# A hybrid SSD and delta-rule layer: the substitution of the 32-blocks and the decay differences on GpSimd instead of VectorE

## The chip, the cores and the metric

One core of one Trainium2 chip runs the whole kernel. The metric is the device time of one execution in microseconds (us); the time before is the median of three executions. All rows below are from one profiled execution. Engine names are those of the profile: PE is TensorE, DVE is VectorE, ACT is ScalarE, POOL is GpSimd, SP is SyncE, whose queue (SPq) issues nearly all DMAs.

## The reference, cut to what matters

The layer projects 1024 latent and 256 context tokens (2048 wide) by `w_in`, runs a depthwise convolution, and feeds half of the width to an SSD scan and half to a gated delta rule with 8 heads of 128, in both directions. The result is normalised and multiplied by `w_out`. The change touches the delta rule alone. In chunks of 128 tokens, for each head and direction:

```python
gcum = jnp.cumsum(g, axis=-1)
decay = jnp.exp(jnp.where(incl, gcum[..., :, None] - gcum[..., None, :], -jnp.inf))
a_strict = jnp.where(strict, jnp.einsum('bhcik,bhcjk->bhcij', k_beta, k) * decay, 0.0)
sol = lax.linalg.triangular_solve(a_strict, rhs, left_side=True, lower=True, unit_diagonal=True)
attn = jnp.einsum('bhcik,bhcjk->bhcij', q, k) * decay
def step(S, inp):
    qd, ke, ui, wi, ai, dec = inp
    v_new = ui - jnp.einsum('bhqk,bhkv->bhqv', wi, S)
    o = jnp.einsum('bhqk,bhkv->bhqv', qd, S) + jnp.einsum('bhqs,bhsv->bhqv', ai, v_new)
    S = S * dec[..., None, None] + jnp.einsum('bhsk,bhsv->bhkv', ke, v_new)
```

There are 10 chunks (8 latent, 2 context), so 20 triangular 128x128 matrices for each head.

## The kernel before, in words

`Layer.build` (L1201) writes the work as a list of steps and issues them in that order. `gdn_block` steps ("g") are convolution blocks: 48 matmuls for each 512 tokens (`group`, L440, L437) into a PSUM bank of the tags d (two) or e (one), then an evacuation by ACT (L490) and four DVE taps (L498), a Tanh (L502) and a DVE product (L503). The weights of a block are split into two float16 halves (L408 to L413), one block ahead. POOL scales the taps (L483).

Head h of the delta rule goes through five steps. "V" (`gdn_post`, L626) normalises. "P" (`gdn_prep`, L679) goes over the 10 chunks: a load `gb<-gr` (L686) brings the cumulated gates of both directions, broadcast over the partitions, into one of four buffers gb; `decay` (L673) subtracts the column's own gate and takes the minimum with the mask `mneg` (0 or -1e30), one DVE instruction for each direction (L676); ACT takes the exponential (L690); PE forms k·k and q·k (L693, L695) in a PSUM bank of the tag m (two); DVE makes A (L697, twice) and the attention block (L700), which is stored from gb (L701), and then gb is free for the next load. After the last chunk `invert_blocks` (L705) sends the 80 diagonal blocks of 32x32 through DRAM so that each lies on one partition (L716, L717, L721), inverts them by substitution, 30 pairs of DVE instructions (L726 a product into tp, L728 a sum into X) each of which needs the one before, writes ones on the diagonal (L729, POOL) and sends them back through DRAM (L730, L732). "I" (`invert`, L735) transposes them (L741, DVE) and builds the 128x128 inverses from them with small matmuls (L764 to L794). "C" (`gdn_chain`, L798) walks the two chains of 10 steps: S·k (L850), r (L856, DVE), the inverse times r (L866), xw (L871, DVE) and r (L873, ACT), the update of S (L876 on PE, L881 on DVE), and the output (L888 on PE, L889 on DVE); vq loads (L811, L813) feed it, and POOL scales finished pairs of outputs (L831 to L835). "E" (`gdn_end`, L895) transposes the output (L96) and stores it.

The order of steps for head h in the loop is P(h+1), C(h), the blocks of head h+2 with E(h) between them, V(h+2), z blocks, I(h+1). Within that, the framework's scheduler merges the steps: each engine's instructions stand in one fixed order, chosen when the program is built from modelled times, and at run time each engine takes them in that order and waits on semaphores. In the trace PE alternates between chain matmuls and matmuls of a convolution block, and DVE between the substitution and the chain.

Of the kernel before, what the change touches and what calls it, by code (L numbers as in the profile page):

```python
# [12 lines left out]
ALU = mybir.AluOpType  # L13

P = 128
# [18 lines left out]
NEG = -1.0e30  # L34
# [10 lines left out]
class Layer:  # L45
# [627 lines left out]
    def decay(self, e, d, h, c):  # L673

        nc = self.nc
        nc.vector.scalar_tensor_tensor(out=e, in0=e, scalar=self.G[:, 32 + d * 8 + h, c:c + 1],  # L676
                                       in1=self.mneg[:, d], op0=ALU.subtract, op1=ALU.min)

    def gdn_prep(self, h, D):  # L679
        nc, sp = self.nc, self.gp  # L680
# [24 lines left out]
    def invert_blocks(self, A):  # L705

        nc, sp = self.nc, self.gp
        t_ = lambda shape, name, **kw: sp.tile(shape, F32, tag=name, name=name, **kw)
        Q = 2 * NCH
        ft = t_([P, NCH, 32], "ft")  # L710
        d1 = self.dram.tile([Q, 4, 32, 32], F32, tag="d1", name="d1", bufs=2)
        d2 = self.dram.tile([Q, 4, 32, 32], F32, tag="d2", name="d2", bufs=2)
        for b in range(4):
            s = slice(32 * b, 32 * b + 32)
            nc.vector.transpose(out=ft[s], in_=A[s, 0, :, s])
            nc.sync.dma_start(out=d1[NCH:, b].rearrange("q j i -> j q i"), in_=A[s, 1, :, s])  # L716
        nc.sync.dma_start(out=d1[0:NCH].rearrange("q b j i -> (b j) q i"), in_=ft)  # L717

        X = t_([P, NCH * P], "X")[0:4 * Q, 0:1024].rearrange("p (a b) -> p a b", b=32)
        tp = t_([4 * Q, 256], "tp")  # L720
        nc.sync.dma_start(out=X, in_=d1.rearrange("q b j i -> (q b) j i"))  # L721
        for k in range(1, 31):
            m = 31 - k
            t = tp[:, 0:m * k].rearrange("p (a b) -> p a b", b=k)
            sh = [4 * Q, m, k]
            nc.vector.tensor_tensor(out=t, in0=X[:, k + 1:, k:k + 1].to_broadcast(sh),  # L726
                                    in1=X[:, k:k + 1, 0:k].to_broadcast(sh), op=ALU.mult)
            nc.vector.tensor_tensor(out=X[:, k + 1:, 0:k], in0=X[:, k + 1:, 0:k], in1=t, op=ALU.add)  # L728
        nc.gpsimd.memset(X.rearrange("p a b -> p (a b)")[:, ::33], 1.0)  # L729
        nc.sync.dma_start(out=d2.rearrange("q b j i -> (q b) j i"), in_=X)  # L730
        xc = t_([P, Q, 32], "xc")
        nc.sync.dma_start(out=xc, in_=d2.rearrange("q b j i -> (b j) q i"))  # L732
        return xc
# [586 lines left out]
```

## Time and profile before

| what | value |
|---|---|
| median of three executions | 2357.67 us (2355.03 to 2359.08) |
| the profiled execution's own time | 2351.73 us |
| span of the profile | 2350.0 us, mean granted TensorE clock 0.978 |
| busy PE / DVE / ACT / POOL | 92% / 60% / 42% / 11% of the span |
| the delta rule's stage (380 to 1480 us) | PE busy 1016.1 of 1100 us, DVE 775.0, ACT 441.7, POOL 160.9 |

A row of a timeline gives the start and the duration in us, engine, line, operation, output<-input, and in brackets the idle time of the engine just before and what ended it. A row of waits says who waited for whom, the us in total, how often, and the longest. A row of a group gives the count, the busy time, the mean ns of one, and the idle time before with its releasers. A row of a stretch gives its bounds and length, then the busy us (and instructions) of PE, PEld (weight loads), DVE, ACT and POOL, then the granted TensorE clock (PEclk, 1.00 is 2.4 GHz, 0.50 is 1.2 GHz), the DMA share and GB/s.

### The profile page before, as it was taken

Reading aid. Unit: us, or ns where it says so; the run is one execution under the profiler, and the core shown is the slowest. Engines: PE = TensorE matmul, PEld = TensorE weight load, DVE = VectorE, ACT = ScalarE, POOL = GpSimd, SP = SyncE. Lnnn points to the kernel's source line nnn. Section 1 sums busy time; section 2 is a strip of 40 time slices with the busy share of each in tenths; the row PEclk is TensorE's granted clock in tenths of the full one; section 3 lists DMA queues with packets and bytes.
Section 4 is the critical chain, followed back from the end, with each engine's and each line's share of the span. In section 5 each row is a group of like instructions: output and inputs, shape, how many; then the busy total and the mean of one; then the engine's idle time right before and its main releaser. Section 6 shows DMA issues by size and latency. Waiting matters only on the chain. (4 is left out here: it accounts for less than half of the span.)

```text
span 2350.0 us, 41855 instructions
## 1 busy us (share of the span) xinstructions
PE 2162.5 (92%) x16070; PEld 1379.2 (59%) x16070; DVE 1399.5 (60%) x3499; ACT 998.5 (42%) x2493; POOL 268.7 (11%) x514
## 2 busy tenths in 40 slices
PE   4989999889999898998989999999999999899998
PEld 4334644456665655556555566555555555788887
DVE  5335543869694856858568486566767773511214
ACT  6026422344444352433524444465667584423320
POOL 1000001012111020111201110130303130000000
PEclk9999999999999999999999999999999999999999
DMA  9952347454444344343443444333465355212117
GB/s 323 348 164 55 80 145 217 117 131 106 134 115 120 101 126 116 88 133 93 121 119 85 127 123 115 99 90 108 111 183 149 98 164 195 68 37 73 55 37 269
DMA packets 397236, 301.71 MB, mean 128 GB/s; under 512 B 61339, under 2 KB 358684, under 8 KB 395628
## 3 DMA queue, kind: packets, MB, share of 16 engines
q1 hardware_dynamic: 386668, 293.80, 43.7%
q10 hardware_dynamic: 10368, 5.24, 0.8%
q8 instruction: 126, 2.06, 0.4%
q14 instruction: 74, 0.61, 0.1%
HBM read 241.41 MB, written 57.57 MB: 127 GB/s over the span
## 5 line engine op out<-in xcount | busy, mean ns | idle before, releaser
L437 PE MATMUL ps_d<-u,w 128*128 128x512 f16 (+1 forms) x4560 | 969.6, 357 | 8.3 <-DVE cv L498 4.6
L437 PEld LDWEIGHTS <-w 128*128 128x128 f16 x6048 | 595.3, 100 | 494.3 <-issue 36.4
L1138 PEld LDWEIGHTS <-u 128*128 128x128 f16 x3072 | 298.7, 98 | 50.9 <-DMA u<-in_w_out_dram 13.2
L437 PE MATMUL ps_e<-u,w 128*128 128x512 f16 (+1 forms) x1296 | 314.5, 376 | 0.0
L498 DVE SCALAR_TENSOR_TENSOR cv<-ps_d,taps,cv 128x496 f32<-128x496 f32 (+3 forms) x300 | 194.8, 650 | 80.0 <-ACT cv L492 38.6
L413 DVE SCALAR_TENSOR_TENSOR w<-w,scl 128x512 f16<-128x512 f32 (+1 forms) x204 | 149.9, 777 | 50.8 <-ACT w L411 50.3
L408 ACT ACTIVATE w<-w 128x1024 f16<-128x1024 f32 (+1 forms) x102 | 106.5, 1044 | 167.7 <-DMA w<-in_w_in_dram 101.5
L1138 PE MATMUL ps_d<-wx,u 128*128 128x256 f16 x1536 | 170.2, 273 | 4.6 <-DMA u<-in_w_out_dram 4.6
L1138 PE MATMUL ps_d<-w,u 128*128 128x256 f16 x1296 | 144.8, 273 | 5.7 <-DMA u<-in_w_out_dram 3.8
L1168 DVE SCALAR_TENSOR_TENSOR raw<-ps_d,inv,gp 128x256 f32<-128x256 f32 x59 | 28.4, 483 | 193.2 <-ACT jko L1166 193.2
L411 ACT ACTIVATE w<-w,scl 128x1024 f16<-128x1024 f32 (+1 forms) x102 | 112.3, 1133 | 36.2 <-DVE scl L145 16.5
L1166 ACT ACTIVATE jko<-ps_d,inv 128x256 f32<-128x256 f32 x59 | 27.8, 471 | 182.4 <-PE ps_d L1138 177.4
L989 ACT ACTIVATE E<-E,G 128x128 f32<-128x128 f32 x256 | 80.9, 388 | 35.1 <-DMA E<-gr 29.6
L690 ACT ACTIVATE gb<-gb 128x256 f32<-128x256 f32 x80 | 32.2, 413 | 147.0 <-DVE gb L676 144.0
L502 ACT ACTIVATE t<-cv 128x512 f32<-128x512 f32 (+1 forms) x98 | 55.7, 570 | 90.0 <-DVE cv L498 75.4
L676 DVE SCALAR_TENSOR_TENSOR gb<-gb,G,mneg 128x128 f32<-128x128 f32 x160 | 50.8, 345 | 69.2 <-DMA gb<-gr 67.9
L873 ACT ACTIVATE r<-ps_c,nb 128x128 f32<-128x128 f32 x128 | 45.7, 364 | 107.0 <-DVE xw L871 97.2
L876 PE MATMUL ps_c<-xw,vq 128*128 128x128 f32 x288 | 61.8, 304 | 30.8 <-DVE xw L871 14.2
L726 DVE TENSOR_TENSOR tp<-X 80x30 f32<-80x30 f32 (+14 forms) x240 | 77.6, 323 | 13.9 <-DMA X<-d 13.2
L876 PEld LDWEIGHTS ps_c<-xw,vq 128*128 128x128 f32 x288 | 47.4, 196 | 58.9 <-ACT r L873 33.7
L503 DVE SCALAR_TENSOR_TENSOR cv<-t,cv 128x512 f32<-128x512 f32 (+1 forms) x98 | 60.5, 618 | 31.7 <-ACT t L502 31.3
L728 DVE TENSOR_TENSOR X<-X,tp 80x30 f32<-80x30 f32 (+14 forms) x240 | 78.4, 327 | 0.6
(329 smaller groups left out, 3250.4 us busy)
## 6 DMA issues: line engine op xcount, KB each, us to landing
w<-in_w_in_dram SPq DMA_DIRECT2D x102, 512.0 KB
x<-in_w_ada_dram SPq DMA_DIRECT2D x48, 1024.0 KB
vq<-vq SPq DMA_DIRECT2D x128, 256.0 KB
E<-gr SPq DMA_DIRECT2D x64, 256.0 KB
u<-in_w_out_dram SPq DMA_DIRECT2D x24, 512.0 KB
gb<-gr SPq DMA_DIRECT2D x80, 128.0 KB
x<-in_x_dram SPq DMA_DIRECT2D x8, 1024.0 KB
vq<-gb SPq DMA_DIRECT2D x64, 128.0 KB
```

What stands on the lines that cost most here:

```text
L408: nc.scalar.activation(out=w16[h][:, 0], in_=w[h], func=AF.Square, accum_out=ssq[:, h:h + 1])
L411: nc.scalar.activation(out=w16[h][:, 0], in_=w[h], func=AF.Copy, scale=t)
L413: nc.vector.scalar_tensor_tensor(out=w16[h][:, 1, s], in0=w[h][:, s], scalar=t, in1=w16[h][:, 0, s], op0=ALU.mult, op1=ALU.subtract)
L437: self.nc.tensor.matmul(out=ps, lhsT=w16[k // KH][:, a, k % KH], rhs=self.u16[b][k][:, lo:lo + n], start=(k == 0 and i == 0), stop=(k == K ...
L498: nc.vector.scalar_tensor_tensor(out=o3[:, :, lo_o:hi_o], in0=p3[:, :, lo_o + s:hi_o + s], scalar=taps[tap], in1=o3[:, :, lo_o:hi_o], op0= ...
L502: nc.scalar.activation(out=t[:, 0:n], in_=o, func=AF.Tanh)
L503: nc.vector.scalar_tensor_tensor(out=o, in0=t[:, 0:n], scalar=1.0, in1=o, op0=ALU.add, op1=ALU.mult)
L726: nc.vector.tensor_tensor(out=t, in0=X[:, k + 1:, k:k + 1].to_broadcast(sh), in1=X[:, k:k + 1, 0:k].to_broadcast(sh), op=ALU.mult)
L728: nc.vector.tensor_tensor(out=X[:, k + 1:, 0:k], in0=X[:, k + 1:, 0:k], in1=t, op=ALU.add)
L876: nc.tensor.matmul(out=pS, lhsT=vq[:, 1], rhs=xw, start=True, stop=True)
L989: nc.scalar.activation(out=E[:, d, r], in_=E[:, d, r], func=AF.Identity, bias=self.G[:, j, c:c + 1])
L1138: self.nc.tensor.matmul(out=ps, lhsT=self.y16(k, p, s), rhs=w16[k // 4][:, q, k % 4], start=(i == 0 and j == 0), stop=(i == KB - 1 and j = ...
```

## The change

`decay` becomes two POOL instructions, a subtraction with a minimum against 0 and an `affine_select` that writes -1e30 beyond the diagonal; and the 60 instructions of each head's substitution are issued on POOL. Nothing else is edited; the DMAs around them stay on SP.

```diff
     def decay(self, e, d, h, c):
         nc = self.nc
-        nc.vector.scalar_tensor_tensor(out=e, in0=e, scalar=self.G[:, 32 + d * 8 + h, c:c + 1],
-                                       in1=self.mneg[:, d], op0=ALU.subtract, op1=ALU.min)
+        nc.gpsimd.tensor_scalar(out=e, in0=e, scalar1=self.G[:, 32 + d * 8 + h, c:c + 1], scalar2=0.0,
+                                op0=ALU.subtract, op1=ALU.min)
+        s = 1 - 2 * d
+        nc.gpsimd.affine_select(out=e, in_=e, compare_op=ALU.is_ge, fill=NEG, base=0, pattern=[[s, P]], channel_multiplier=-s)
...
-            nc.vector.tensor_tensor(out=t, in0=X[:, k + 1:, k:k + 1].to_broadcast(sh),
+            nc.gpsimd.tensor_tensor(out=t, in0=X[:, k + 1:, k:k + 1].to_broadcast(sh),
                                     in1=X[:, k:k + 1, 0:k].to_broadcast(sh), op=ALU.mult)
-            nc.vector.tensor_tensor(out=X[:, k + 1:, 0:k], in0=X[:, k + 1:, 0:k], in1=t, op=ALU.add)
+            nc.gpsimd.tensor_tensor(out=X[:, k + 1:, 0:k], in0=X[:, k + 1:, 0:k], in1=t, op=ALU.add)
```

## Rows read from the trace of the kernel before

**Rows 1.** The page, part 1: busy time, share and instructions of each engine.
```profile
PE 2162.5 (92%) x16070; PEld 1379.2 (59%) x16070; DVE 1399.5 (60%) x3499; ACT 998.5 (42%) x2493; POOL 268.7 (11%) x514
```

**Rows 2.** Busy time by stretch, around the prep and the substitution of one head.
```profile
750.00:790.00 40.00, 31.78 (x197) 22.54 (x195) 27.38 (x83) 8.57 (x21) 0.00 (x0) 0.96 0.50 127
790.00:830.00 40.00, 38.84 (x238) 26.85 (x239) 36.78 (x129) 14.25 (x40) 10.19 (x24) 0.96 0.27 77
```

**Rows 3.** Waits of PE in the delta rule's stage, 380 to 1480 us.
```profile
PE ps_c L888 <- DVE S L881: 14.4, 7, 3.3
PE ps_c L876 <- DVE xw L871: 14.2, 5, 3.2
PE ps_c L876 <- ACT r L873: 13.4, 8, 3.0
PE ps_c L876 <- DMA vq<-gb: 3.0, 1, 3.0
```

**Rows 4.** Groups of DVE instructions that the change moves.
```profile
L728 DVE TENSOR_TENSOR X<-X,tp 80x30 f32<-80x30 f32 (+14 forms) x240 | 78.4, 327 | 0.6
L726 DVE TENSOR_TENSOR tp<-X 80x30 f32<-80x30 f32 (+14 forms) x240 | 77.6, 323 | 13.9 <-DMA X<-d 13.2
L676 DVE SCALAR_TENSOR_TENSOR gb<-gb,G,mneg 128x128 f32<-128x128 f32 x160 | 50.8, 345 | 69.2 <-DMA gb<-gr 67.9 <-issue 1.2
```

**Rows 5.** Timeline of DVE: a gb wait, and the substitution's first and last instructions.
```profile
759.47 0.61 DVE L676 SCALAR_TENSOR_TENSOR gb<-gb,G,mneg 128x128 f32<-128x128 f32 x2 [3.17 <-DMA gb<-gr]
760.00 0.60 DVE L871 TENSOR_SCALAR xw<-ps_c,pw 128x128 f32<-128x128 f32 x2
...
790.65 0.20 DVE L726 TENSOR_TENSOR tp<-X 80x30 f32<-80x30 f32 x1 [2.90 <-DMA X<-d]
790.77 0.33 DVE L881 SCALAR_TENSOR_TENSOR S<-S,cd,ps_c 128x128 f32<-128x128 f32 x1
...
825.56 0.18 DVE L728 TENSOR_TENSOR X<-X,tp 80x30 f32<-80x30 f32 x1
```

**Rows 6.** Timeline of PE: waits behind the X load, first and last of five.
```profile
655.65 0.49 PE L888 MATMUL ps_c<-r,vq 128*128 128x128 f32 x2 [1.37 <-DVE S L881]
...
1228.23 0.79 PE L888 MATMUL ps_c<-r,vq 128*128 128x128 f32 x2 [2.65 <-DVE S L881]
```

**Rows 7.** Busy time and granted clock (PEclk) after the last of those waits.
```profile
1230.00:1234.00 4.00, 4.00 (x21) 3.44 (x20) 2.40 (x8) 1.74 (x4) 0.00 (x0) 0.50 0.46 129
```

**Rows 8.** Timeline of POOL: operations of two sizes, and their spacing.
```profile
502.53 0.61 POOL L664 TENSOR_TENSOR cv<-cv,kn 128x256 f32<-128x256 f32 x1
...
546.93 0.20 POOL L831 TENSOR_TENSOR ss<-ss,s 128x2 f32<-128x2 f32 x1 [41.68 <-ACT jk L829]
547.22 0.24 POOL L832 TENSOR_SCALAR ss<-ss 128x2 f32<-128x2 f32 x1
```

**Rows 9.** Groups of POOL instructions with one tensor input.
```profile
L654 POOL TENSOR_SCALAR nrm<-nrm 128x8 f32<-128x8 f32 x8 | 2.1, 267 | 0.7
L112 POOL TENSOR_SCALAR_AFFINE_SELECT mneg<-mneg 128x128 f32<-128x128 f32 x2 | 0.5, 292 | 0.0
```

**Rows 10.** Timeline of ACT: an exponential that waits for the decays.
```profile
774.08 0.42 ACT L690 ACTIVATE gb<-gb 128x256 f32<-128x256 f32 x1 [3.92 <-DVE gb L676]
```

**Rows 11.** Timelines: where the blocks' inverse is used, head 3 (first two) and head 0.
```profile
836.83 0.83 DVE L741 STREAM_TRANSPOSE xt<-xc 128x640 f32<-128x640 f32 x1
...
882.44 0.22 PE L764 MATMUL ps_m<-xc,A 32*32 32x32 f32 x2
...
477.63 0.25 PE L764 MATMUL ps_m<-xc,A 32*32 32x32 f32 x4 [1.21 <-DMA xc<-d]
```

**Rows 12.** Timelines of DVE and POOL: two instructions that overlap.
```profile
673.54 0.82 DVE L728 TENSOR_TENSOR X<-X,tp 80x238 f32<-80x238 f32 x1
...
673.49 0.61 POOL L835 TENSOR_TENSOR o<-o,ss 128x256 f32<-128x256 f32 x1
672.73 0.40 DVE L726 TENSOR_TENSOR tp<-X 80x238 f32<-80x238 f32 x1
```

## The prediction, made before the changed kernel ran

> **What bounds the kernel now.** I read the page's busy times first: PE is busy for 92% of the span, DVE for 60%, POOL for 11% [rows 1]. So an instruction taken from DVE is worth only the PE idle time that it causes. The delta rule's stage holds both moved parts; PE is busy there for 1016 of 1100 us (table of times), and 84 us idle are all that could be won, beside the clock. Next I read the busy times by stretch, to see where in a head that idle lies. While the prep runs (750 to 790 us) PE is busy for 31.8 of 40 us; while the substitution runs (790 to 830) for 38.8 of 40, with DVE at 36.8 [rows 2]. The substitution's load on DVE therefore costs PE almost nothing; the prep's waits cost it 8 us a head. Last I read PE's waits in that stage by releaser, and the timeline around them [rows 3, 5]. Each engine takes its instructions in a fixed order, and what PE waits for is mostly a short chain operation on DVE or ACT that stands behind one that waits for a DMA. Two places repeat from head to head. (a) The chain's xw (L871) stands behind a decay (L676) that waited 3.17 us for its gb load [rows 5]. (b) The state's update S (L881) stands behind the substitution's first product (L726), which waited 2.90 us for X from DRAM; the two products and S run within 0.5 us of the landing [rows 5]. On ACT the exponential (L690) waits 3.92 us for a decay, and the chain's r (L873) follows it [rows 10].
>
> **What leaves DVE.** 50.8 + 78.4 + 77.6 = 207 us of busy time [rows 4], so DVE comes to about 1193 us, 51% of the span. Of this the substitution's share is 156 / 8 = 19.5 us a head, in a stretch where PE is idle for 1.2 of 40 us [rows 2]: I price it at 0, with 8 x 1.2 = 9 us as the most it could give.
>
> **The X wait, (b).** It happens in five heads, 13.2 us of DVE idle time in all [rows 4]. PE's waits for S right behind it run from 1.37 to 3.31 us; the five are 1.37, 2.47, 1.14, 3.31 and 2.65, together 10.9 of the 14.4 us for S [rows 3, 6]. After the change POOL waits for X. What stands behind on POOL is the chain's scaling of outputs and a block's taps; neither is in PE's next microseconds, so this wait goes: -11 us. After the last of the five the granted clock stood at 0.50 (1.2 GHz) for at least 4 us [rows 7], which hold 2 us of work at 1.00 (2.4 GHz); the stretch of the second has a mean of 0.96 over 40 us [rows 2], 1.6 us. So -4 us more for these two.
>
> **The gb wait, (a).** L676 waited 67.9 us for gb in all [rows 4]. PE's share of it is 14.2 us behind xw, 3.0 in the head where the row names the vq load (there too DVE stood at L676 until 759.47, xw started at 760.00 [rows 5]), and the 14.4 - 10.9 = 3.5 left of S: 20.7 us. DVE's wait moves to POOL, but the next instruction on DVE, A (L697), needs the exponential of the same decays. xw is free; what stands behind L697 (mostly S) now meets the wait instead. And the wait gets longer. POOL's subtraction on 128x128 isn't in the trace: below is 0.27 us (the same operation on 8 columns), above 0.61 (a two-input operation on 256 columns) [rows 8, 9]. I take 0.37, near the 0.29 of an affine_select of this very size, which also has one tensor input. The spacing of dependent POOL instructions adds 0.09 (547.22 - 546.93 - 0.20) [rows 8]. One chunk is then 2 x (0.37 + 0.29 + 0.18) = 1.7 us against 0.61 on DVE [rows 5], so each late exponential comes 1.1 us later. I take half of the 20.7 as saved (-10), and 1.1 us added at each of some 6 waits of PE for ACT's r (8 of them, 13.4 us [rows 3]): +6. Together -4 us, between -20.7 (L697 blocks nothing) and +14 (all seven DVE waits return 1.1 us longer, +7.7, and the +6).
>
> **The substitution on POOL.** From 2 to 256 columns POOL's two-input operation goes from 0.20 to 0.61 us, 1.61 ns a column [rows 8]. A head has 30 pairs on (31-k) x k columns, 9920 in all: 16.0 us, with 60 x 0.20 fixed and 60 x 0.09 spacing, 33 us. On DVE it took 825.74 - 790.65 = 35.1 us, since chain operations stand between [rows 5]. So it ends at the same time, unless small strided rows cost POOL more. No POOL row has them; between nothing and half more per instruction I take nothing, and keep 47 us as the upper end. The Trainium skill (GPSIMD Engine Reference, Performance versus the Vector engine) gives 4497 ns for a two-input operation on 2048 columns, which is 2.2 ns a column; by that estimate the substitution would take 39 us and the sum would be 6 us higher at each place without slack. In the middle heads the result is read by PE at 882.44, 57 us after the last sum [rows 5, 11], and this cover is convolution matmuls. In head 0 PE already waits 1.21 us for xc [rows 11], and the last head likewise ends close: 2 us each, +4 us. If the cover fails in the middle heads too, DVE stops first, at the transpose L741, 11 us behind the last sum [rows 5, 11].
>
> **Queues.** POOL grows by 8 x 33 + 80 x 1.7 = 400 us to about 28% of the span, so it doesn't become the bound. Its other work (taps, scaling of outputs) stands between substitution instructions as the chain's stands on DVE now, up to half a microsecond late each time: 0, covered by the free PSUM banks and by the distance from L835 to the transposes of E. The DMA of X back (L730) waits on SP for the same last sum; the weight loads behind it move with it, by 0 in the sum. No DMA is issued from POOL.
>
> **The sum.** -11 - 4 - 4 + 4 = -15 us on the profiled execution's 2351.73 us, which is 5.9 us under the median of the runs. On the median that is 2357.67 - 15 = 2343 us.
>
> **The rivals.** (1) *Both waits go.* The order that is chosen anew puts all the chain's work ahead of L697, and DVE no longer stands between a DMA and the chain: -11 - 4 - 20.7, and the slow clock behind the gb waits, about as much per wait as in (b) (2 us for 2 or 3 of them, -5), make 41 us with no more than +4 back: 2357.67 - 37 = 2320 us. For it: L676 is the only cause of xw's wait. Against: L697 follows at once and has the same source.
> (2) *Late decays, slower than before.* The round of the four gb buffers (load, decay, exponential, A, store, next load) is what paces the prep. Six chunks of a head follow in three rounds, and each round grows by 1.1 to 2.2 us, the second where both chunks land together. If PE's order doesn't cover it, that is 3.3 to 6.6 us a head, 5 in the middle, 40 us over 8 heads, in place of the +6 counted in (a): -15 - 6 + 40 = +19 us, 2377 us. For it: PE stands for 8 of 40 us in this very stretch [rows 2], and ACT's r waits eight times [rows 3]. Against: the order is made anew with POOL in it, and can put convolution matmuls into the longer rounds. It decides from about 2 us added per head and more.
> (3) *The substitution ends late.* DVE and POOL hold each other up: a sum on DVE of 0.40 us took 0.82 while POOL's 0.61 us operation ran [rows 12]. The substitution on POOL would meet the weight splits (L413) and L503 in the same way. With the strided rows it then takes 47 us; the first and the last head wait 12 us each in place of 2, so -15 + 20 = +5 us, 2363 us. The Trainium skill (SBUF — State Buffer, Who interferes with whom) states that a DVE instruction with two SBUF inputs and a GpSimd one that reads SBUF exclude each other for a whole instruction; the trace agrees, 0.42 us lost in one sum beside L835, and by that rule alone this rival has its chance. That the instructions stay on DVE is no rival, since the engine is written out at each call.
>
> **How the numbers follow.** The forecast has 0.42, rival (1) 0.17, rival (2) 0.24, rival (3) 0.17. A measurement of this kernel tells 0.2%, about 4.7 us, from no change. The forecast's own range, by the bounds of (a) and of the +4, is 2325 to 2361; so of its 0.42 I count 0.34 as faster, 0.06 as the same and 0.02 slower. Rival (1) is faster throughout, (2) slower but for 0.02, and (3) splits 0.07 the same, 0.10 slower. That makes faster 0.51, same 0.15, slower 0.34. For 8 in 10 the range goes from 2312, just below rival (1), to 2385, just above rival (2).
>
> **What would show it.** In the changed kernel's profile: DVE near 1190 us and POOL near 670; no DVE idle time put down to the X load, and none of PE's waits for S beside it; 33 to 36 us from the first to the last L726 instruction on POOL; POOL's decays at 0.37 and 0.29 us; ACT's L690 waiting for POOL about 1 us longer each time; PE busy for more than 31.8 of the 40 us of a prep. The prediction is wrong if PE's waits in the prep grow (rival 2), if they vanish (rival 1), or if PE or DVE waits for xc in more heads than the first and the last (rival 3).

## The result and the profile after

The changed kernel is slower, by far more than any case of the prediction: 2582.46 us (median of four, 2578.40 to 2590.33) against 2358.38 us for the kernel before on the same chip, a ratio of 1.0953, 95% interval 1.0918 to 1.0988. That is 224 us; the forecast was -15. Lines of the changed kernel stand two further on from L679 (the transpose L741 is L743, r on ACT is L875, and so on); in the experiments they stand up to four further on.

The page of the changed kernel, part 1 as in [rows 1], and PE's row of part 2 (busy tenths in 40 slices of 64.4 us):

```profile
PE 2209.7 (86%) x16070; PEld 1399.6 (54%) x16070; DVE 1262.7 (49%) x2859; ACT 996.9 (39%) x2493; POOL 662.3 (26%) x1314
...
PE   5989998679869778697698696899999999999998
```

POOL gained 394 us of busy time, near the 400 that were forecast. DVE lost 137 and not the 207 that were subtracted: records of DVE overlap at their ends (in [rows 5] a product that started at 790.65 lasts 0.20 us and S starts at 790.77), and busy time counts an overlap once. But PE, which computes exactly what it did, is idle for 2576.7 - 2209.7 = 367 us, against 2350.0 - 2162.5 = 187.5 before, and is busy 47 us longer, since its mean granted clock fell from 0.978 to 0.941. So of the 226.7 us by which the span grew, 179.5 are idle time of PE and 47.2 a slower clock behind it. The sixes and sevens of PE's row lie in the delta rule's stage.

The groups of POOL instructions that the change made (as [rows 4]):

```profile
L676 POOL TENSOR_SCALAR gb<-gb,G 128x128 f32<-128x128 f32 x160 | 115.6, 734 | 192.3 <-DMA gb<-gr 147.7
...
L730 POOL TENSOR_TENSOR X<-X,tp 80x30 f32<-80x30 f32 (+14 forms) x240 | 130.3, 543 | 17.1
L728 POOL TENSOR_TENSOR tp<-X 80x30 f32<-80x30 f32 (+14 forms) x240 | 121.4, 506 | 40.9 <-DMA X<-d 23.7
```

The substitution's instructions have a mean of 0.52 us, where 0.47 was worked out; the subtraction takes 0.73 us and not 0.37. Even with nothing beside them these differences don't come to 224 us: 160 x 0.36 = 58 us for the subtractions, and some 36 us for the eight substitutions, which take 36.5 to 40.7 us from the first product to the last sum where 33 was worked out. The waits of PE from 380 to 1700 us (as [rows 3]):

```profile
PE ps_c L878 <- ACT r L875: 132.3, 27, 20.1
PE ps_c L854 <- DMA vq<-vq: 38.4, 2, 19.5
PE ps_c L852 <- DVE S L883: 28.4, 7, 4.4
PE ps_m L766 <- DMA xc<-d: 22.9, 1, 22.9
```

The longest of the first row is 20.1 us and of the second 19.5; before, no wait of PE for these was longer than 3.3 [rows 3]. The timeline has one such wait of 17.7 to 20.1 us in each of the heads 2 to 7, 116 us together, and head 0 has the 22.9 us of the last row; head 1's longest is 7.2. Here is head 3's: POOL's last sum, then the queue of SP, then ACT, DVE and PE:

```profile
913.31 0.24 POOL L730 TENSOR_TENSOR X<-X,tp 80x30 f32<-80x30 f32 x1
913.51 0.19 POOL L833 TENSOR_TENSOR ss<-ss,s 128x2 f32<-128x2 f32 x1
...
913.58 0.32 SPq L732 DMA_DIRECT2D d<-X  x1
...
916.43 0.37 SPq L734 DMA_DIRECT2D xc<-d  x1
...
901.18 0.37 ACT L875 ACTIVATE r<-ps_c,nb 128x128 f32<-128x128 f32 x1 [0.23 <-DVE xw L873]
920.28 0.93 ACT L749 COPY A<-xc 32x320 f32<-32x320 f32 x2 [18.73 <-DMA xc<-d]
921.23 0.37 ACT L875 ACTIVATE r<-ps_c,nb 128x128 f32<-128x128 f32 x1
...
920.28 0.84 DVE L743 STREAM_TRANSPOSE xt<-xc 128x640 f32<-128x640 f32 x1 [16.40 <-DMA xc<-d]
...
921.65 0.79 PE L878 MATMUL ps_c<-xw,vq 128*128 128x128 f32 x2 [17.70 <-ACT r L875]
```

Read it from below. PE waits 17.70 us for an r of the chain of head 2. ACT could have made that r long ago, but the instruction ahead of it in ACT's fixed order is a copy of the step "I" of head 3 (L749), and that one waits 18.73 us for xc, the blocks' inverse of head 3 on its way back from DRAM. DVE stands at the transpose L743 for the same load (16.40 us). The load was issued at 916.43, behind the store of 913.58, behind POOL's last sum. So the chain of head 2, which needs nothing from head 3, waits for head 3's substitution. In the kernel before, the first of these copies starts at 835.57, behind the chain's last r at 824.40, and nothing of the chain is held (ACT's timeline of that kernel):

```profile
824.40 0.37 ACT L873 ACTIVATE r<-ps_c,nb 128x128 f32<-128x128 f32 x1 [1.29 <-PE ps_c L866]
...
835.57 0.46 ACT L747 COPY A<-xc 32x320 f32<-32x320 f32 x1 [0.89 <-DMA xc<-d]
```

The busy time around the wait, with the columns of [rows 2], shows what else it costs, a mean granted clock of 0.80:

```profile
880.00:920.00 40.00, 23.74 (x153) 17.36 (x151) 18.74 (x53) 9.55 (x25) 33.74 (x64) 0.80 0.24 60
```

The waits of all engines over the whole span say the same in sums, and show the second matter, the exponential that waits for POOL (before, it waited 144.0 us for DVE in 49 waits):

```profile
ACT gb L692 <- POOL gb L679: 218.3, 72, 13.3
...
ACT A L749 <- DMA xc<-d: 145.2, 7, 24.3
...
DVE xt L743 <- DMA xc<-d: 109.7, 8, 21.9
```

### The profile page after: what moved, and what is told of

Same layout as the page of the kernel before. It is cut to its first block, busy times and chain, and to the rows that moved or that the text cites. A ratio compares the mean times of both kernels' runs of the same rounds, so it can differ in the third digit from the quotient of the medians.

```text
span 2576.7 us, 42245 instructions
## 1 busy us (share of the span) xinstructions
PE 2209.7 (86%) x16070; PEld 1399.6 (54%) x16070; DVE 1262.7 (49%) x2859; ACT 996.9 (39%) x2493; POOL 662.3 (26%) x1314
## 4 chain that ended last, share of the span: by engine, by line
PE 40%; DMA 14%; POOL 13%; ACT 6%; DVE 5%; issue 5%; SPq 1%; POOLq 0%; DVEq 0%; ACTq 0%
PE ps_d L437 17%; PE ps_d L1140 11%; PE ps_e L437 5%; POOL X L730 5%; POOL tp L728 5%; DMA gb<-gr 4%; DMA E<-gr 2%; DMA vq<-gb 1%; DMA u<-in_w_out_dram 1%; ACT E L991 1%; DMA xc<-d 1%; POOL gb L676 1%; DMA y<-p 1%; DVE w L413 1%; DMA d<-X 1%
## 5 line engine op out<-in xcount | busy, mean ns | idle before, releaser
L437 PE MATMUL ps_e<-u,w 128*128 128x512 f16 (+1 forms) x1296 | 324.3, 384 | 3.5 <-DVE cv L498 3.5
L413 DVE SCALAR_TENSOR_TENSOR w<-w,scl 128x512 f16<-128x512 f32 (+1 forms) x204 | 153.1, 791 | 56.5 <-ACT w L411 56.2
L676 POOL TENSOR_SCALAR gb<-gb,G 128x128 f32<-128x128 f32 x160 | 115.6, 734 | 192.3 <-DMA gb<-gr 147.7
L730 POOL TENSOR_TENSOR X<-X,tp 80x30 f32<-80x30 f32 (+14 forms) x240 | 130.3, 543 | 17.1
L728 POOL TENSOR_TENSOR tp<-X 80x30 f32<-80x30 f32 (+14 forms) x240 | 121.4, 506 | 40.9 <-DMA X<-d 23.7
L699 DVE SCALAR_TENSOR_TENSOR A<-gb,nb,ps_m 128x128 f32<-128x128 f32 x160 | 48.9, 344 | 95.0 <-ACT gb L692 84.0
L483 POOL TENSOR_SCALAR taps<-cw_gdn,inv 128x5 f32<-128x5 f32 x24 | 8.6, 357 | 337.3 <-DVE inv L160 314.7
```

The source lines that it names most:

```text
L413: nc.vector.scalar_tensor_tensor(out=w16[h][:, 1, s], in0=w[h][:, s], scalar=t, in1=w16[h][:, 0, s], op0=ALU.mult, op1=ALU.subtract)
L437: self.nc.tensor.matmul(out=ps, lhsT=w16[k // KH][:, a, k % KH], rhs=self.u16[b][k][:, lo:lo + n], start=(k == 0 and i == 0), stop=(k == K ...
L676: nc.gpsimd.tensor_scalar(out=e, in0=e, scalar1=self.G[:, 32 + d * 8 + h, c:c + 1], scalar2=0.0, op0=ALU.subtract, op1=ALU.min)
L728: nc.gpsimd.tensor_tensor(out=t, in0=X[:, k + 1:, k:k + 1].to_broadcast(sh), in1=X[:, k:k + 1, 0:k].to_broadcast(sh), op=ALU.mult)
L730: nc.gpsimd.tensor_tensor(out=X[:, k + 1:, 0:k], in0=X[:, k + 1:, 0:k], in1=t, op=ALU.add)
```

## The experiments

Three theories stood after this profile. A: the order. The scheduler plans the changed program anew, puts instructions that need the substitution's result ahead of the chain's last steps, and in-order queues (ACT, DVE, SP, PE) stop there until POOL is done. B: the late decays, rival (2), in larger size. C: DVE and POOL hold each other up, rival (3). All ratios are to the kernel before on the same chip, and expectations stand as written before each run.

**One part alone.** The first takes the two decay instructions back to DVE, the second takes the substitution back:

```diff
-        nc.gpsimd.tensor_scalar(out=e, in0=e, scalar1=self.G[:, 32 + d * 8 + h, c:c + 1], scalar2=0.0,
-                                op0=ALU.subtract, op1=ALU.min)
...
-        nc.gpsimd.affine_select(out=e, in_=e, compare_op=ALU.is_ge, fill=NEG, base=0, pattern=[[s, P]], channel_multiplier=-s)
+        nc.vector.scalar_tensor_tensor(out=e, in0=e, scalar=self.G[:, 32 + d * 8 + h, c:c + 1],
+                                       in1=self.mneg[:, d], op0=ALU.subtract, op1=ALU.min)
```

```diff
-            nc.gpsimd.tensor_tensor(out=t, in0=X[:, k + 1:, k:k + 1].to_broadcast(sh),
+            nc.vector.tensor_tensor(out=t, in0=X[:, k + 1:, k:k + 1].to_broadcast(sh),
...
-            nc.gpsimd.tensor_tensor(out=X[:, k + 1:, 0:k], in0=X[:, k + 1:, 0:k], in1=t, op=ALU.add)
+            nc.vector.tensor_tensor(out=X[:, k + 1:, 0:k], in0=X[:, k + 1:, 0:k], in1=t, op=ALU.add)
```

> The substitution on GpSimd, the decays on VectorE as before. Theory A (order): ACT's copies of xc into A and DVE's transpose of xc stand ahead of the chain's last operations, the substitution ends later than that order supposes, and PE waits some 18 us a head behind them: these waits stay in seven heads, 2490 to 2530 us. Theory B (late decays): the loss comes from the decays' 0.71 + 0.29 us, so this kernel is near the one before, 2340 to 2370 us. Theory C (lock): DVE's two-input operations (L413, L503) are held up beside the substitution; their mean rises by more than 20% and PE's waits are many and short, about 2500 us.

> The decays on GpSimd, the substitution on VectorE as before. A: the long waits for xc are gone and what is left is the later exponential, 2390 to 2440 us. B: nearly all of the loss stays, 2530 to 2590 us. C: nearly none of it, 2355 to 2380 us.

Substitution alone: 2536.41 us, ratio 1.0761 (1.0730 to 1.0792). Decays alone: 2413.94 us, ratio 1.0251 (1.0219 to 1.0283). Both parts lose. The two losses (7.6% and 2.5%) add up to 10.1%, a little over the 9.5% of the whole; the intervals only just meet. The first time lies 6 us above theory A's range, the second within it. With the substitution alone each head has one PE wait of 17 to 25 us. Again the same load holds ACT at the copy and DVE at the transpose; but what PE waits for in heads 3 to 6 is now DVE's output sum (L889), which stands behind the transpose (timeline of that kernel, ACT, DVE and PE in head 4):

```profile
1070.99 1.39 ACT L747 COPY A<-xc 32x320 f32<-32x320 f32 x3 [23.78 <-DMA xc<-d]
...
1070.94 0.85 DVE L741 STREAM_TRANSPOSE xt<-xc 128x640 f32<-128x640 f32 x1 [22.80 <-DMA xc<-d]
1071.71 0.25 DVE L889 TENSOR_TENSOR o<-ps_c,o 128x128 f32<-128x128 f32 x1
...
1072.02 0.80 PE L850 MATMUL ps_c<-S,cv 128*128 128x128 f32 x2 [22.47 <-DVE o L889]
```

With the decays alone there is no wait of PE over 5 us in this stage, but many of 2 to 4 us. PE's waits in that kernel:

```profile
PE ps_c L878 <- ACT r L875: 46.1, 21, 4.2
...
PE ps_c L852 <- DVE S L883: 21.7, 6, 4.3
```

One of them in its timeline, POOL then ACT then PE:

```profile
794.40 1.40 POOL L676 TENSOR_SCALAR gb<-gb,G 128x128 f32<-128x128 f32 x2 [5.72 <-DMA gb<-gr]
795.76 0.54 POOL L679 TENSOR_SCALAR_AFFINE_SELECT gb<-gb 128x128 f32<-128x128 f32 x2
...
796.33 0.42 ACT L692 ACTIVATE gb<-gb 128x256 f32<-128x256 f32 x1 [5.02 <-POOL gb L679]
796.65 0.35 ACT L875 ACTIVATE r<-ps_c,nb 128x128 f32<-128x128 f32 x1
...
797.05 0.79 PE L878 MATMUL ps_c<-xw,vq 128*128 128x128 f32 x2 [4.07 <-ACT r L875]
```

The gb wait, which DVE had, is POOL's now; but the exponential behind it waits for the same load and for 1.9 us of POOL's work besides, and the chain's r is next on ACT. The wait has moved from xw to r and has grown. PE is busy for 26.18 of the 40 us around it, at a clock of 0.87 (busy time by stretch; [rows 2] had 31.78 at 0.96 for a prep):

```profile
780.00:820.00 40.00, 26.18 (x128) 17.57 (x129) 18.24 (x54) 9.73 (x25) 18.78 (x40) 0.87 0.42 106
```

**The order held on ACT and DVE.** If the order alone is at fault, instructions of "I" that are kept behind the end of the head before, on ACT and DVE, must take the long waits away. The whole change (e3), and the substitution alone (e4), with this edit (`ac` and `dv` are the last ACT and DVE instructions of "E"):

```diff
+        self.ends = (ac.ins, dv.ins)
...
             elif k == "I":
-                self.invert(heads[m]["T"], heads[m]["xc"])
+                with ExitStack() as q:
+                    for i in getattr(self, "ends", ()):
+                        q.enter_context(self.tc.issue_after(i))
+                    self.invert(heads[m]["T"], heads[m]["xc"])
```

> Both parts on GpSimd as in the change; only the order is held: the instructions of the step that builds the 128x128 inverses are queued on ACT and DVE behind the end of the same iteration's output step, so behind the whole chain. A: PE's waits of 17 to 20 us behind ACT's copies go in six heads (about 110 us of idle and some 20 us of slow clock): 2430 to 2470 us. B and C: nothing that costs time is touched, 2570 to 2600 us.

> The substitution on GpSimd with the order held as in e3, the decays on VectorE. A: the substitution then costs only what the first head waits for xc and gains the waits behind X: 2340 to 2380 us. B: 2340 to 2370 us, as without the held order. C: above 2450 us, since the two engines still exclude each other.

Whole change: 2558.63 us, 1.0857 (1.0829 to 1.0885); substitution alone: 2524.42 us, 1.0720 (1.0690 to 1.0750). Both are a miss for theory A as it stood: only 1.0% and 0.4%, some 23 and 10 us, came back, and the second is within the noise (the intervals of e1 and e4 overlap). But the wait for the copies had gone, and a new one stood in its place, for vq: 13.6 to 19.5 us in heads 2 to 7 of e3, 17.2 to 23.7 in heads 1 to 7 of e4. Timeline of e4, head 4, SP's queue and PE:

```profile
1030.07 6.11 SPq L813 DMA_DIRECT2D vq<-vq  x3
1060.07 0.33 SPq L730 DMA_DIRECT2D d<-X  x1
1060.49 0.38 SPq L394 DMA_DIRECT2D w<-in_w_in_dram  x1
1062.96 0.37 SPq L732 DMA_DIRECT2D xc<-d  x1
1063.42 2.54 SPq L813 DMA_DIRECT2D vq<-vq  x2
...
1068.05 0.80 PE L852 MATMUL ps_c<-S,vq 128*128 128x128 f32 x2 [22.39 <-DMA vq<-vq]
```

SP issues DMAs in a fixed order too. The store of X (L730) waits there for POOL, and the chain's own loads of vq (L813) stand behind it: nothing from about 1036 to 1060 us. The same fault on another queue: with ACT and DVE opened, SP held.

**The order held on SP as well.** e6 is e4 with the two return DMAs issued in "I", and queued behind the last vq load of the chain:

```diff
-        nc.sync.dma_start(out=d2.rearrange("q b j i -> (q b) j i"), in_=X)
...
-        nc.sync.dma_start(out=xc, in_=d2.rearrange("q b j i -> (b j) q i"))
-        return xc
+        return X, d2, xc
...
+        X, d2, xc = xc
+        nc.sync.dma_start(out=d2.rearrange("q b j i -> (q b) j i"), in_=X)
+        nc.sync.dma_start(out=xc, in_=d2.rearrange("q b j i -> (b j) q i"))
...
+        self.ends = (ac.ins, dv.ins, self.lastvq)
```

> As e4, and the two DMAs that bring the substitution's result back through DRAM are traced in the later step and queued on SP behind the chain's last vq load. Theory A, widened (every in-order queue that holds something waiting for the substitution stops the chain: in e1 DVE and ACT, in e4 SP): the seven waits of 17 to 24 us for vq go, about 150 us of idle; what remains is the first head's wait of 22 us: 2355 to 2395 us. Rival D (the longer substitution itself is what the next chain waits for, so that the wait only moves on to PE's matmuls of the inverse or to the next chain's first step): 2480 to 2530 us, with PE waiting for xc or A in most heads. Theory C (lock): no change from e4, 2510 to 2530 us.

2368.25 us, ratio 1.0076 (1.0059 to 1.0093). Of the 7.2% of e4, 6.4 are gone, with the substitution on POOL as before. This settles where the larger part of the loss came from: not from the substitution's duration, which is 37 to 39 us a head in this kernel too, but from what stood behind its result. PE's waits that are left in it beyond those of the kernel before:

```profile
PE ps_m L765 <- DMA xc<-d: 23.2, 1, 23.2
...
PE ps_c L96 <- POOL o L836: 16.1, 5, 10.3
```

The first is head 0, where little work lies between the substitution and its use; the second, 3.4 us before, is mostly in head 6, whose last scaling of outputs on POOL (L836) is queued behind head 7's substitution. The waits for S beside the X load have gone.

**The decays.** Two experiments on e2 ask why the decays lose. e7 leaves the minimum against 0 out of the subtraction (`scalar2=None`, one operation), e8 has six buffers gb instead of four (`GB = 6`).

> As e2 (decays alone on GpSimd), with the minimum against 0 left out of the subtraction, so that it has one operation; what lies beyond the diagonal is overwritten by the select in any case. If the second operation is what makes 0.71 us of the 0.37 that was estimated, the subtraction falls to 0.35 to 0.45 us and the time to 2385 to 2400 us. If it is the scalar read from SBUF or the engine's rate for this operation, it stays at 0.65 to 0.75 us and 2405 to 2420 us.

> As e2, with six buffers gb in place of four, so that a round of load, decay, exponential, A and store paces six chunks. If the loss of e2 is the longer round, most of it comes back: 2360 to 2390 us, with DVE's and ACT's waits behind the decays halved. If it is the later exponential by itself, wherever it stands, 2405 to 2420 us.

One operation: 2400.76 us, 1.0219 (1.0199 to 1.0239). Six buffers: 2407.42 us, 1.0243 (1.0223 to 1.0262). The subtraction's rows in e2 and in e7 (min, median and max in ns):

```profile
L676 POOL TENSOR_SCALAR gb<-gb,G x160: 705/712/1727, 396.9 to 1416.1; 128x128 f32<-128x128 f32 x160
```

```profile
L676 POOL TENSOR_SCALAR gb<-gb,G x160: 597/602/1494, 394.6 to 1402.9; 128x128 f32<-128x128 f32 x160
```

The second operation costs 0.11 us of 0.71, so the one-input subtraction with a scalar from SBUF is 0.60 us by itself, between the two cases that were expected. Taking 0.22 us off a chunk gave back 0.3% or so, two intervals that overlap. More buffers gave nothing that can be told, so the round of the buffers is not what limits; with six the waits only stood elsewhere (27.3 us for gb from L702, 21.1 for r). What is left as the cause is the later exponential on ACT, wherever it stands; that was seen in the timeline, not isolated by a run of its own.

**Head 0, the whole change, and a control.** e9 is e6 with "I" of head 0 one convolution block later and held behind it on PE, ACT, DVE and SP; e10 adds the decays on POOL, so it is the whole change with the order held; e11 is the kernel before with the same hold and nothing on POOL.

```diff
-        steps = gdn(0) + [("P", 0)] + gdn(1)[:1] + [("I", 0)] + gdn(1)[1:] + z(12)
+        steps = gdn(0) + [("P", 0)] + gdn(1)[:2] + [("I", 0)] + gdn(1)[2:] + z(12)
...
-                    for i in getattr(self, "ends", ()):
+                    for i in self.ends if m else self.ends0:
```

> As e6, and the first head's inverse is queued behind the next convolution block on PE, ACT, DVE and SP, so that PE has that block to do while the substitution runs. Theory A: the wait of 23 us for xc in the first head goes too, and against the kernel before the waits of S behind the X load are gone: 2330 to 2350 us, beside some 2350 for the kernel before. Rival D (the substitution's length is needed by someone in any case): PE waits for xc or for A in another place of the first head, and the time stays at 2360 to 2370 us.

> The change whole, decays and substitution on GpSimd, with the order held as in e9. If the two parts' costs stand side by side, the substitution's goes and the decays' 58 us stay: 2395 to 2425 us. If the decays' later exponential also delays the substitution so far that the held order no longer covers it, above 2450 us with waits for xc or A.

> The kernel before, both parts on VectorE, with the order held as in e9: the control. If holding the order brings something by itself, whatever engine the substitution runs on, this one is faster than the kernel before by 10 us or more. If not, it is within 8 us of it, and what e9 gains comes from the substitution's place.

e9: 2374.23 us, 1.0089 (1.0069 to 1.0109), a miss: head 0 still waits 23.2 us for xc. The edit did not reach its aim. PE's trace has 2799 matmuls ahead of the first use of xc in e9, the same as in e6 and in the changed kernel, where the kernel before has 2878; so whether one block more would cover the wait was not tried, and e9 is in effect e6 again. e10: 2453.02 us, 1.0413 (1.0390 to 1.0436). e11: 2346.52 us, 0.9977 (0.9965 to 0.9990). So holding the order takes 5.4 of the whole change's 9.5%, and it does next to nothing for the kernel before: the hold repairs what the change broke and is no gain of its own. With the order held, the decays are worth 4.13 - 0.89 = 3.2%, the larger part of what remains and more than the 2.5% that they cost alone. e10 fits neither case of its expectation: it lies above 2450 us, but head 0 alone waits for xc, 22.4 us as in e9; what grew are PE's waits for r (52.4 us) and S (27.7 us) of the chain. Why the decays cost more here was not taken apart.

**The two ends of the row of heads.** e12 is e9 with heads 0 and 7 substituted on DVE again:

```diff
+        eng = nc.gpsimd if 1 <= h <= 6 else nc.vector
...
-            nc.gpsimd.tensor_tensor(out=t, in0=X[:, k + 1:, k:k + 1].to_broadcast(sh),
+            eng.tensor_tensor(out=t, in0=X[:, k + 1:, k:k + 1].to_broadcast(sh),
...
-            nc.gpsimd.tensor_tensor(out=X[:, k + 1:, 0:k], in0=X[:, k + 1:, 0:k], in1=t, op=ALU.add)
+            eng.tensor_tensor(out=X[:, k + 1:, 0:k], in0=X[:, k + 1:, 0:k], in1=t, op=ALU.add)
```

> The kernel with the substitution on POOL and the inverse's instructions held back on PE, ACT, DVE and SP (0.89% slower than the kernel before), with one edit: heads 0 and 7 are substituted on DVE again, heads 1 to 6 stay on POOL; the decays are on DVE. Theory A (what is left of the loss is two places alone: PE's 23.2 us for xc in head 0, and PE's 14 us for POOL's scaling of o in head 6, behind head 7's substitution): both waits go, about 2374 - 23 - 14 = 2337 us, ratio 0.992 to 0.997, at or below the control's 0.9977, in which all eight heads are on DVE. Theory B (POOL's substitution costs the middle heads too, by DVE and POOL locking each other): 6 of 8 of what is left stays, 2374 - 7 = 2367 us, ratio 1.004 to 1.008.

2341.35 us against 2360.17, ratio 0.9918 (0.9899 to 0.9936): theory A. This is 0.8% faster than the kernel before and, by the ratios, 0.6% faster than the control, the lowest ratio of all kernels here. Its page, part 1, and PE's waits for S and for xc:

```profile
PE 2159.1 (92%) x16070; PEld 1374.4 (59%) x16070; DVE 1325.1 (57%) x3139; ACT 995.7 (43%) x2493; POOL 458.7 (20%) x874
```

```profile
PE ps_c L891 <- DVE S L884: 3.2, 5, 2.3
...
PE ps_m L767 <- DMA xc<-d: 1.1, 1, 1.1
```

The same wait for S in the control e11, with all substitutions on DVE:

```profile
PE ps_c L890 <- DVE S L883: 12.8, 6, 3.7
```

Of the 12.8 us of the control, 9.1 stand right behind DVE's wait for X, in heads 2 to 6; in e12 POOL has that wait, and none of PE's waits for S is there. Theory C falls as a cause of the loss: with six substitutions on POOL the time went down, and the weight splits of L413 have a median of 746 or 747 ns in the kernels before, after and here. Medians hide single cases, though. DVE's instructions that are in both kernels take 12.7 us more in e12 than in e11, added up, and a POOL sum on 240 columns or fewer took up to 1.18 us where the shortest on 240 takes 0.64. So the two engines may well hold each other up now and then; no wait of PE showed it.

## Why the prediction was wrong, step by step

**What bounds the kernel: right.** PE is the bound, DVE's relief beyond the X wait bought nothing that shows, and places where one engine stands between a DMA and the chain decide. It was the application that stopped short. (DVE's 51% was a wrong reading of the rows, as said above, and changed nothing in the sum.)

**The X wait, -15 with the clock: right, and seen only in e12.** In the changed kernel it is buried. Against its control e12 gains 0.9977 - 0.9918 = 0.6%, 14 us by the ratios; between the two profiled executions it is 8.4 us, 5.3 of them idle time of PE and 3.1 busy time. All five heads that had the wait are among the six on POOL. The waits for S behind X that went are 9.1 us, where 10.9 were forecast.

**The substitution on POOL: duration right, price wrong. This is the step that failed.** From the first product to the last sum it takes 36.5 to 37.4 us in heads 2 to 6 of the changed kernel (40.7 in head 1), between the 33 taken and the upper end of 47, and some 2 us more than on DVE. So the duration was good enough. The estimate by the Trainium skill (GPSIMD Engine Reference, Performance versus the Vector engine), from 4497 ns for 2048 columns, was 39 us; the trace agrees within 3 us. The step then read the cover from the old order: "57 us after the last sum", "this cover is convolution matmuls". But the order is part of what the change makes. In the new program the copies, the transpose and the two DMAs that need the result stand ahead of the chain's last steps, and the cover was the chain. e1, e4 and e6 show it: 7.6% with the order as planned, 7.2% with two queues opened, 0.8% with all. The step's last sentence named the place, "DVE stops first, at the transpose L741", should the cover fail in the middle heads, but put no price on it: the term for these heads was 0, and the runs showed a wait of 17.7 to 20.1 us in each of the heads 2 to 6.

**"Queues: 0": wrong, the same step from the other side.** It looked for what stands between POOL's instructions and for the weight loads on SP behind L730. It did not ask what else ACT, DVE and SP hold behind an instruction that waits for xc. In e4 SP alone holds the chain's vq loads for 17 to 24 us a head. And L835 had a price: 16.1 us in e6 against 3.4 before, 10.3 of them one wait where head 6's outputs stand behind head 7's substitution, not "up to half a microsecond late each time".

**The first and the last head, 2 us each: wrong by size.** Head 0 waits 22.9 us for xc in the changed kernel, 1.21 before [rows 11]. The last sum of head 0 came at 481.4 and not at 471.1, 10.3 us later; the other 11.4 us are work that no longer stands ahead of the use in the new order: 2799 matmuls and 399.0 us of PE's busy time, where 2878 and 410.5 stood before. e12, with head 0 on DVE, has 2878 again and waits 1.1 us. In the last head PE's wait is the 19.5 us for vq.

**The decays, -4: wrong by size and sign.** The subtraction was taken at 0.37 us "near the 0.29 of an affine_select of this very size, which also has one tensor input"; it is 0.71, above the upper bound of 0.61. The nearest rows were of the same operation, TENSOR_SCALAR, at 2 and 8 columns [rows 8, 9], and a bound from a two-input operation did not bound it. A chunk takes 1.93 us in the timeline of e2 (794.40 to 796.33), against the 1.7 worked out, so this size is the smaller part of the error: with 2 x (0.60 + 0.29) = 1.8 us e7 still lost 2.2%. The larger part is what a late exponential was said to cost, +6 us at six waits and nothing for the clock. In e2 PE waits 46.1 us for r in 21 waits, where it was 13.4 in 8 [rows 3]; the waits for xw have gone, but the half of the 20.7 us that was to be saved is more than eaten up; PE's idle time grew by 32.0 us, and its busy time by another 31.2 at a mean granted clock of 0.964. The mechanism seen is the late decays of rival (2), with ACT's r behind the exponential, at 2.5% or some 58 us alone, where rival (2) had 40; e8 shows that it is not by the round of four buffers, as rival (2) had it.

**The rivals.** (1) had the decays' wait vanish; the measured sign is the opposite. (2) is a true part in its place, if not in its round of buffers: 2.5% alone and 3.2% with the order held, a quarter to a third of the loss. (3) had named the sign of what came, waits for xc in more heads than the first and the last, but it had the wrong cause and priced two heads only: in e12 six substitutions on POOL show no cost in the sum. The Trainium skill (SBUF — State Buffer, Who interferes with whom) has a DVE instruction with two SBUF inputs contend with a GpSimd one that reads SBUF, by an exclusive lock; the trace agrees in single cases, 0.82 us for a sum that took about 0.40 otherwise [rows 12].

**What stays open.** Why the planner set the copies so early is not shown: that it counts POOL's instructions as shorter than they run would explain it, and was not tried. The decays' loss was not taken apart beyond e7 and e8, nor was its growth in e10; and no run covered the wait of head 0 with the substitution on POOL.

## What to carry to other kernels

When an operation is moved to another engine in a program whose order is made by a scheduler, the cover that the old trace shows is not the cover that the new program has: list every in-order queue (engines and DMA issuers) that will hold an instruction waiting for the moved result, and what stands behind it there. If a slow producer cannot be hurried, hold back its consumers on all of those queues at once, since with one opened the next one can stop for about as long. Move an operation only where there is other work beside it: here the six middle heads gained 0.6% on POOL (e12 against e11), and the first and the last lost 1.7% (e9 against e12).

## What the runs showed of the hardware that was not expected

A POOL TENSOR_SCALAR on 128x128 with its scalar from SBUF takes 0.60 us with one operation and 0.71 with two, twice to two and a half times the 0.29 us of an affine_select of the same size on the same engine. Strided rows cost POOL little: the shortest substitution instructions on 80x30 to 80x240 elements took 0.23 to 0.64 us in the changed kernel, where the whole-row operations of [rows 8] would give 0.25 to 0.59. And a stalled PE paid twice here: in the changed kernel 179.5 us of idle time came with 47.2 us of longer busy time at a lower granted clock, in e2 32.0 with 31.2.
